# Output projection of a hybrid attention block: another pairing of the heads, and product 2 of both column blocks ahead of the rest

## The chip, the cores and the metric

The kernel runs on one core of one Trainium2 chip. The metric is the device time of one execution in microseconds (us). TensorE (PE) multiplies, VectorE (DVE) and ScalarE (ACT) do the elementwise work, GpSimd (POOL) a little masking, and SyncE (SP) issues the DMAs.

## What is computed

One layer of a hybrid encoder block in float32, for 512 tokens of width 2048: an input projection, eight heads of stick-breaking attention, eight heads of forgetting attention, a norm of each head, the output projection, and an MLP. The change lies in the output projection; cut to that, the reference is:

```python
o_sb = stick_breaking_attention(qa, ka, va)            # heads 0..7
o_fox = forgetting_attention(qf, kf, vf, log_f)        # heads 8..15
mixed = concatenate([head_rmsnorm(o_sb, g_out_sb), head_rmsnorm(o_fox, g_out_fox)], axis=-1)
x = x + einsum('bse,ed->bsd', mixed, w_out)            # (512 x 2048) @ (2048 x 2048)
h2 = rmsnorm(x, g_mlp)
u = relu(einsum('bsd,df->bsf', h2, w_up))
x = x + einsum('bsf,fd->bsd', u * u, w_down)
y = rmsnorm(x, g_final)
```

## The kernel before, in words

Every float32 product is made of three matmuls on fp32r halves (`mm3`, lines 77 to 79): high x high, high x low, low x high. The high half is a cast on ACT, the low half a subtraction on DVE (`split`, lines 59 and 60).

The large products are done as 2 x 2 blocks with seven products in place of eight (Strassen's scheme in Winograd's form), numbered 1 to 7. For the output projection the left matrix `mixed` (tokens x heads) is split into two token halves and two inner halves, and w_out into the same inner halves and two column halves. Before, the inner halves are the even heads and the odd heads: a pair `m` holds heads 2m and 2m+1. Product 1 is A11 B11 and reads the first inner half alone, product 2 is A12 B21 and reads the second half alone, product 4 also reads only the second, and products 5, 6, 7 and 3 need both or sums of them. The sums of the weights for products 4 to 7 are made during attention (`WeightSums`, line 986 loads two row blocks of w_out for each m) and kept in DRAM (`wsums`, `whigh`; the ready halves of products 1 and 2 for column block 0 in `wraws`).

The left forms are made by `g_form(p, parts)`: sums on DVE in place in `mixed`, a cast on ACT, a subtraction on DVE, over the pairs m0 to m1. They lie in tiles `G[p]` that take over rooms of the earlier input tiles; the left forms `F` of the next stage take over those rooms again (`left_form`).

A column half of 1024 is done in two column blocks of 512 (`db` 0 and 1). In each block every product runs in four pieces of two pairs (`out_piece(p, db, m0)`), 12 matmuls of 512 columns each. The weights of a piece come into a pair of buffers (high and low): three pairs in the pool `w`, and in column block 0 a fourth (`px`), in turn. For column block 0 of products 1 and 2 they are loaded ready (line 1410), for product 6 half ready (lines 1412 and 1413), for all others loaded raw (lines 1431 and 1433) and split on ACT and DVE.

The sums are gathered in three accumulators in PSUM, `A`, `B` and `C`, each of two tiles of 512. In the trace they are accoa, accob and accoc. Products 1, 6, 7 and 4 add up in one accumulator, 5 and 3 in C; `take(p, db)` (line 1453) adds an accumulator to a quarter of x on DVE after each product that ends a value, and product 6 goes on adding onto product 1 behind such a take. Before, in column block 0, A is accoa and B, for product 2, is accob; in block 1 they are exchanged. `turn_quarter` then transposes the finished quarter on TensorE (line 1460).

PSUM pools are opened and closed like a stack: in attention `acca` (two tiles of 512), `accb` (two) and the pool of the scores, whose tile `s` has 1536 floats, with one more tile of 512. For the output projection accoa, accob and accoc are opened in that order, at the same starts. The last values of the heads are summed in `accb` (`accv`), and the output and the norm sums of the last head lie in a tile `oq` of the scores' tag.

Attention runs the forgetting heads first and the stick-breaking heads last; heads 6 and 7 are the last two. Their chain at the end is: transposes of the weights (line 885), product with the values (lines 77 to 79 on `o` and `oq`), squares, norm sums (lines 956 and 957), a reciprocal root on ACT (lines 960 and 961), four operations on DVE (lines 966 to 969) which write `mixed`. Before, all that doesn't need heads 6 and 7 is product 1 and product 2 of block 0 without their piece m0 = 2 (pairs 2 and 3): six pieces, put behind steps of that chain by `issue_after`. Then the rest follows in the order 1, 2, 6, 5, 7, 3, 4.

The order inside attention is written out by hand; in the output projection it is that of the code, except that a planner puts an instruction ahead where an earlier one isn't ready by its own reckoning. On the chip each engine runs its own list in order.

Of the kernel before, what the change touches and what calls it, by code (L numbers as in the profile page):

```python
# [8 lines left out]
F32 = mybir.dt.float32  # L9
# [6 lines left out]
P = 128  # L16
NT = 512
# [3 lines left out]
NH = 8  # L21
# [16 lines left out]
def block_kernel(ctx, tc, x, g_attn, w_in, b_f, g_out_sb, g_out_fox, w_out, g_mlp, w_up, w_down, g_final, y):  # L38
# [5 lines left out]
    w_in, w_out, w_up, w_down = w_in[0], w_out[0], w_up[0], w_down[0]  # L44
# [84 lines left out]
    A_ORDER = (1, 4, 5, 6, 2, 7, 3)  # L129
    ROOMS = [f"f{c}{p}" for c in "hl" for p in A_ORDER]  # L130
# [90 lines left out]
    with ExitStack() as stage:  # L221
# [70 lines left out]
        c0, m = v_columns(order[0]), 2 * P + NH  # L292
# [82 lines left out]
        for k in range(4, K8):  # L375
            t, j = mm_at[k], k + K8
# [334 lines left out]
    mixed = mixp.tile([P, 2 * NH, NT], F32, name="mixed")  # L711
# [3 lines left out]
    with tc.tile_pool(name="att", bufs=1, side="right", reuse_waits="tile") as at, \  # L715
# [259 lines left out]
        class WeightSums:  # L975
# [4 lines left out]
            def load(self, sides=(0, 1)):  # L980
                if 0 in sides:
                    self.b = self.place()
                    self.q = [self.b[:, i] for i in range(4)]
                for s in sides:
                    src = w_out[(2 * self.m + s) * P:(2 * self.m + s + 1) * P].rearrange("p (j c) -> p j c", j=2)
                    sp.dma_start(self.b[:, 2 * s:2 * s + 2], src[:, :, self.ds[0] * NT:self.ds[0] * NT + self.n])

            def high(self, i):
# [209 lines left out]
    class form:  # L1198
        @staticmethod
        def tile(*args, tag, **kwargs):  # L1200
            return (form1 if tag in EARLY else form2).tile(*args, tag=tag, **kwargs)

    G_ORDER = (1, 2, 6, 5, 7, 3, 4)


    G = {p: [form.tile([P, NH, 2 * P], F32R, tag=ROOMS[2 * i + c], name=f"g{p}") for c in range(2)]
         for i, p in enumerate(G_ORDER)}
    F = {p: [None, None] for p in A_ORDER}

    def f_parts(p, a):  # L1210
# [31 lines left out]
    def a_form(p, c, out, s=None):  # L1242
        split(*out, a_source(p, c, s))
# [144 lines left out]
    aps, bps, cps = (ops.enter_context(tc.tile_pool(name=f"{c}ps", bufs=1, space=PSUM, reuse_waits="tile")) for c in "abc")  # L1388

    A, B, C = (q.tile([P, 2, NT], F32, name=f"acco{c}") for c, q in zip("abc", (aps, bps, cps)))  # L1390
    A, B = (A, B), (B, A)
    S_OF = xp.tile([P, NH, 2 * P], F32, tag="hr1", name="s12")
    out_rows = w_out.rearrange("(m s p) c -> s p m c", s=2, p=P)

    def g_form(p, *parts):
        for m0, m1 in parts:
            a_form(p, mixed[:, 2 * m0:2 * m1].rearrange("p (m s) n -> p m s n", s=2), [g[:, m0:m1, :] for g in G[p]])

    def parts_at(pool_, tag):
        t_ = pool_.tile([P, 2, 2 * NT], F32R, tag=tag, name="wx")  # L1400
# [5 lines left out]
    def out_piece(p, db, m0):  # L1406

        hi, lo = (w.rearrange("p (a b) -> p a b", a=2) for w in hi_lo(2 * NT))
        if db == 0 and p in (1, 2):
            begun_ = [sp.dma_start(w.bitcast(F32), wraws[p - 1][:, m0 // 2, i]) for i, w in enumerate((hi, lo))][1]  # L1410
        elif db == 0 and p == 6:
            begun_ = sp.dma_start(hi.bitcast(F32), whigh[:, m0 // 2])
            sp.dma_start(lo.bitcast(F32), wsums[:, m0 // 2, 3, db])
        else:
            raw = out_weights(p, db, m0)
            casts[0] = split(hi, lo, raw[0])
            begun_ = raw[1]
        ps = {2: B[db], 5: C, 3: C}.get(p, A[db])
        for t in range(2):
            ts = slice(t * P, (t + 1) * P)  # L1420
            for i in range(2):
                mm3(ps[:, t, :], G[p][0][:, m0 + i, ts], G[p][1][:, m0 + i, ts], hi[:, i, :], lo[:, i, :],
                    m0 + i == 4 and p in (1, 5, 2), m0 + i == 3)
        return begun_

    def out_weights(p, db, m0):
# [13 lines left out]
    def begin(t, j, db):  # L1440

        if t + j + db == 0:

            quarter[t, j] = wp.tile([P, 2, NT], F32, tag="wraw", name="x2")
        else:
            quarter[t, j] = xp.tile([P, 2, NT], F32, tag="x2", name="x2", bufs=3)
        sp.dma_start(quarter[t, j], xq[:, 2 * t:2 * t + 2, (2 * j + db) * NT:(2 * j + db + 1) * NT])

    def take(p, db):
        q, ps = {1: ((0, 0), A[db]), 5: ((1, 1), C), 6: ((0, 1), A[db]), 2: ((0, 0), B[db]), 7: ((1, 1), A[db]),  # L1450
                 3: ((0, 1), C), 4: ((1, 0), A[db])}[p]
        for t in range(2) if p == 4 else [slice(0, 2)]:
            dve.tensor_tensor(quarter[q][:, t, :], quarter[q][:, t, :], ps[:, t, :], op=ALU.add)
# [14 lines left out]
    def turn_quarter(t0, j, db):  # L1468
        n = 2 * j + db
        x_ = quarter[t0, j]  # L1470
        if hr[db][j] is None:
            hr[db][j] = xp.tile([P, 2, 2, NT], F32, tag=f"hr{j}", name="hr")
        for a in range(2):
            take_group(t0, j, db, a, turn_group(t0, j, db, a))
        sp.dma_start(xd[n][:, 2 * t0:2 * t0 + 2, :], x_)
        squares.append((t0, n, x_))
# [14 lines left out]
            F[p][db] = form.tile([P, 4, 2, 2 * P], F32R, tag=f"f{'hl'[db]}{p}", name=f"f{p}")  # L1491
        a_form(p, hr[db][j], [F[p][db][:, 2 * j:2 * j + 2, c, :] for c in range(2)])

    pending = []
    for db in range(2):
        if db == 1:
            begin(0, 0, db)
        else:

            for p in (1, 2):  # L1500
                g_form(p, (4, 8), (0, 2), (2, 3))
            with tc.issue_after(last_heads[2].ins):
                for p in (4, 5):
                    g_form(p, (4, 8), (0, 2), (2, 3))
            more_parts.append(lambda: parts_at(px, "px"))
            out_piece(1, 0, 4)
            with tc.issue_after(last_heads[3].ins):
                out_piece(1, 0, 6)
            with tc.issue_after(last_heads[2].ins):
                with tc.issue_after(last_heads[0].ins):  # L1510
                    out_piece(1, 0, 0)
                    out_piece(2, 0, 4)
                with tc.issue_after(last_heads[1].ins):
                    out_piece(2, 0, 6)
                    out_piece(2, 0, 0)
            begin(0, 0, db)
            for p in (1, 2, 4, 5):
                g_form(p, (3, 4))
            g_form(6, (4, 6), (6, 8), (0, 2), (2, 4))
            last_heads[4] = lows[0]  # L1520
        for i, p in enumerate(G_ORDER):
            for m0 in (2,) if db == 0 and p in (1, 2) else (4, 6, 0, 2):
                ins = out_piece(p, db, m0)
                if pending:

                    with tc.issue_after(casts[0].ins), tc.issue_after(lows[0].ins):
                        left_form(*pending.pop(0))
                if (db or p in (3, 4)) and m0 in (6, 2) and first_loads:

                    with tc.issue_after(ins.ins):  # L1530
                        u, k, a = first_loads.pop(0)
                        units[u].load(k, a)
                if db == 0 and p in (6, 5, 7) and m0 == 2:

                    with tc.issue_after(ins.ins):
                        begin(*{6: (0, 1), 5: (1, 1), 7: (1, 0)}[p], db)
                if db == 0 and p in (6, 5) and m0 != 4:

                    with tc.issue_after(last_heads[4].ins):
                        g_form({6: 7, 5: 3}[p], {6: (4, 8), 0: (0, 2), 2: (2, 4)}[m0])  # L1540
            if db == 0 and p == 5:
                more_parts.pop()
                px_cm.__exit__(None, None, None)
                mixp_cm.__exit__(None, None, None)
                rw = ctx.enter_context(tc.tile_pool(name="rw", bufs=5, side="right", reuse_waits="tile"))
                units += [Unit(0), Unit(1)]
            if db == 1 and p == 2:
                begin(0, 1, db)
                begin(1, 1, db)
            if db == 1 and p == 3:  # L1550
                begin(1, 0, db)
            take(p, db)
            if db == 1:
                pending += [(q, 0, j) for q in A_ORDER[2 * i:2 * i + 2] for j in range(2)]
            if len(squares) > 0:

                with ExitStack() as order_:
                    if casts[0] is not None:
                        order_.enter_context(tc.issue_after(casts[0].ins))
                    take_squares()  # L1560
            if p in (2, 7, 3):
                turn_quarter(*{2: (0, 0), 7: (1, 1), 3: (0, 1)}[p], db)
            if db == 1 and p == 6:
                left_form(1, 1, 0)
            if db == 1 and p == 3:
                left_form(1, 1, 1)
                for j in range(2):
                    left_form(2, 1, j)
                for q in (4, 5, 6):
                    left_form(q, 1, 1)  # L1570
        if db == 1:
            with tc.issue_after(lows[0].ins):
                summed[7, 1, 1] = a_source(7, hr[1][1])
            with tc.issue_after(casts[0].ins):
                begun = [units[0].parts(1), units[0].parts(2)]
            for p in (5, 7):
                units[0].sum_ahead(p)
        else:
            turn_quarter(1, 0, db)
# [583 lines left out]
```

## Time and profile before

| what | value |
|---|---|
| timed runs | 2003.61, 2003.64 and 2004.72 us; median 2003.64 |
| profiled execution | span 2002.0 us from the first to the last instruction; the page gives no time of its own beside it |
| busy | PE 1993.2, PE weight loads 1727.1, DVE 1745.6, ACT 1202.3, POOL 63.3 us |
| granted clock of TensorE | 0.999 on average |
| DMA | 423.54 MB, 212 GB/s on average |
| output projection in the trace | from 585 to 760 us |

In the rows below, the first number of a timeline is the start in us from the span's start, the second the duration. Then come the engine, the line of the kernel, the operation and the tiles (output<-inputs), the shape, how many instructions the row merges (x), and in brackets how long the engine was idle before it and who ended that. PEld is the loading of a matmul's stationary operand, SPq SyncE's queue of DMAs. A stretch row gives for each engine the busy time and the number of instructions, then the granted clock, the share of DMA time and the rate.

### The profile page before, as it was taken

To read this page: it belongs to the slowest core of one execution; us is meant where nothing else is said; L and a number is where in the kernel's file an instruction comes from. 1 tells how busy PE (TensorE), PEld (TensorE's weight loads), DVE (VectorE), ACT (ScalarE), POOL (GpSimd) and SP (SyncE) were. 2 spreads that over 40 slices of the span, in tenths; PEclk is the share of its full clock that TensorE was granted. 3 is DMA by queue.
4 is the path that set the end of the run, shared out by engine and by line. 5 is a ranking of instruction groups with operands and counts; after the bars stand their busy time and mean duration, and the time that the engine had idled before them with its cause. 6 is when DMAs were issued, how large, how long until landed. Compare 5 with 4: busy or idle time off the path is not lost.

```text
span 2002.0 us, 27075 instructions
## 1 busy us (share of the span) xinstructions
PE 1993.2 (100%) x10288; PEld 1727.1 (86%) x10288; DVE 1745.6 (87%) x1997; ACT 1202.3 (60%) x1648; POOL 63.3 (3%) x73
## 2 busy tenths in 40 slices
PE   9999999999999999999999999999999999999998
PEld 9998888888898889888888888888888888888887
DVE  7886888888878678999999999998798888988896
ACT  7544766787765566767676776766543444344344
POOL 0000011010110000000000000000000000000003
PEclk9999999999999999999999999999999999999999
DMA  7417977777668962666766666666694674674642
GB/s 262 157 65 246 292 230 212 227 225 219 212 214 279 299 221 95 200 203 199 219 184 215 199 203 201 199 211 233 245 348 165 228 279 142 239 262 171 215 163 85
DMA packets 309570, 423.54 MB, mean 212 GB/s; under 512 B 49424, under 2 KB 205376, under 8 KB 302912
## 3 DMA queue, kind: packets, MB, share of 16 engines
q1 hardware_dynamic: 308688, 419.71, 63.9%
q10 hardware_dynamic: 752, 2.11, 0.3%
q8 instruction: 81, 1.33, 0.3%
q14 instruction: 49, 0.40, 0.1%
HBM read 315.45 MB, written 96.49 MB: 206 GB/s over the span
## 4 chain that ended last, share of the span: by engine, by line
PE 100%; DVE 0%; issue 0%; DVEq 0%; ACT 0%; ACTq 0%
PE psa L1313 11%; PE accd L79 8%; PE accd L77 8%; PE accd L78 8%; PE accq L77 6%; PE accq L78 6%; PE accq L79 6%; PE psa L1311 6%; PE psc L1313 5%; PE psc L1311 3%; PE psb L1313 3%; PE psb L1311 1%; PE m L79 1%; PE m L77 1%; PE m L78 1%; PE accoa L77 1%
## 5 line engine op out<-in xcount | busy, mean ns | idle before, releaser
L1949 ACT CAST wh<-wd 128x1024 fp32r<-128x1024 f32 x126 | 125.0, 998 | 168.2 <-PE accd L79 55.3
L1835 DVE TENSOR_TENSOR wl<-wu,wh 128x1024 fp32r<-128x1024 f32 x158 | 192.6, 1219 | 12.2 <-ACT wh L1829 12.0
L77 PE MATMUL accq<-hH,wh 128*128 128x512 f32 x512 | 200.3, 391 | 0.0
L78 PE MATMUL accq<-hL,wh 128*128 128x512 f32 x512 | 199.4, 389 | 0.0
L79 PE MATMUL accq<-hH,wl 128*128 128x512 f32 x512 | 199.4, 389 | 0.0
L1829 ACT CAST wh<-wu 128x1024 fp32r<-128x1024 f32 x158 | 167.6, 1061 | 44.0 <-issue 27.9
L1313 PE MATMUL psa<-f,wh 128*128 128x512 f32 x720 | 179.0, 391 | 0.0
L79 PE MATMUL accd<-wh,uf 128*128 128x512 f32 x436 | 169.6, 389 | 0.0
L78 PE MATMUL accd<-wl,uf 128*128 128x512 f32 x436 | 169.6, 389 | 0.0
L77 PE MATMUL accd<-wh,uf 128*128 128x512 f32 x436 | 169.5, 389 | 0.0
L1313 PEld LDWEIGHTS psa<-f,wh 128*128 128x128 f32 x720 | 132.3, 188 | 25.6
L1956 DVE TENSOR_TENSOR wl<-wd,wh 128x1024 fp32r<-128x1024 f32 x126 | 143.9, 1150 | 10.6 <-ACT wh L1949 10.6
L1949 ACT CAST wx<-wd 128x1024 fp32r<-128x1024 f32 (+1 forms) x82 | 80.8, 994 | 107.4 <-PE accd L79 43.6
L1670 DVE TENSOR_TENSOR m<-m,accd 128x1024 f32<-128x1024 f32 x84 | 102.1, 1216 | 47.9 <-PE accd L79 47.9
L79 PEld LDWEIGHTS accq<-hH,wl 128*128 128x128 f32 x512 | 96.1, 188 | 20.3
L77 PEld LDWEIGHTS accq<-hH,wh 128*128 128x128 f32 x512 | 96.2, 188 | 19.0
L78 PEld LDWEIGHTS accq<-hL,wh 128*128 128x128 f32 x512 | 96.2, 188 | 18.9
L77 PE MATMUL accd<-wx,uf 128*128 128x512 f32 x284 | 110.5, 389 | 0.0
L78 PE MATMUL accd<-wx,uf 128*128 128x512 f32 x284 | 110.5, 389 | 0.0
L79 PE MATMUL accd<-wx,uf 128*128 128x512 f32 x284 | 110.5, 389 | 0.0
L1311 PEld LDWEIGHTS psa<-f,wl 128*128 128x128 f32 x720 | 96.0, 191 | 5.4
L1311 PE MATMUL psa<-f,wl 128*128 128x256 f32 x720 | 98.3, 282 | 0.0
(464 smaller groups left out, 5120.5 us busy)
## 6 DMA issues: line engine op xcount, KB each, us to landing
wu<-in_w_up_dram SPq DMA_DIRECT2D x60, 1024.0 KB, 6.5
ufd<-st SPq DMA_DIRECT2D x98, 512.0 KB, 4.2
wd<-in_w_down_dram SPq DMA_DIRECT2D x48, 1024.0 KB, 8.4
uf<-ufd SPq DMA_DIRECT2D x42, 1024.0 KB, 7.5
wraw<-in_w_in_dram SPq DMA_DIRECT2D x68, 512.0 KB, 5.7
wo<-wsums SPq DMA_DIRECT2D x28, 512.0 KB, 4.7
q<-in_w_in_dram SPq DMA_DIRECT2D x32, 384.0 KB, 5.3
wd<-in_w_down_dram SPq DMA_DIRECT2D x16, 768.0 KB, 5.8
```

The lines of the kernel that those rows point to most:

```text
L77: pe.matmul(out, sh, mh, start=first, stop=False, skip_group_check=True)
L78: pe.matmul(out, sh, ml, start=False, stop=False, skip_group_check=True)
L79: return pe.matmul(out, sl, mh, start=False, stop=last, skip_group_check=True)
L1311: ins = pe.matmul(ps[:, 2 * P:], lo[:, a, :], f_parts(p, a)[0], start=False, stop=last, skip_group_check=True)
L1313: ins = pe.matmul(ps, hi[:, a, :], f_both(p, a), start=a == PAIRS[0] and p in (1, 5), stop=last, skip_group_check=True)
L1670: dve.tensor_tensor(M[p][:, :, db, :], M[p][:, :, db, :], ps, op=ALU.add)
L1829: act.copy(rooms[k][0], srcs[k])
L1835: lows[0] = dve.tensor_tensor(lo, srcs.pop(k), hi.bitcast(F32), op=ALU.subtract)
L1949: act.copy(rooms[k + 3][0], srcs[k + 3])
L1956: dve.tensor_tensor(rooms[k + 2][1], srcs.pop(k + 2), rooms[k + 2][0].bitcast(F32), op=ALU.subtract)
```

## The change

The inner halves are now the stick-breaking heads (first) and the forgetting heads (second): pair m holds heads m and 8 + m. So product 2 (and 4) reads forgetting heads only, and product 1 stick-breaking heads only. Product 2 is done for both column blocks ahead of everything else, in accoa for block 0 and in accoc for block 1; product 1 of block 0 goes to accob, with its pairs 0 to 5 ahead of the last heads and the piece m0 = 6 (heads 6 and 7) behind them. The pieces run in the order m0 = 0, 2, 4, 6. Products 1, 6, 5, 7, 3, 4 follow. A quarter of x for block 1 takes product 2's result at once and is kept in a room of product 2's left form. The left forms of the next stage and the loads of w_up are spread over the new order.

```diff
-                    src = w_out[(2 * self.m + s) * P:(2 * self.m + s + 1) * P].rearrange("p (j c) -> p j c", j=2)
+                    src = w_out[(s * NH + self.m) * P:(s * NH + self.m + 1) * P].rearrange("p (j c) -> p j c", j=2)
...
-    G_ORDER = (1, 2, 6, 5, 7, 3, 4)
+    G_ORDER = (1, 6, 5, 7, 3, 4)
     G = {p: [form.tile([P, NH, 2 * P], F32R, tag=ROOMS[2 * i + c], name=f"g{p}") for c in range(2)]
-         for i, p in enumerate(G_ORDER)}
+         for i, p in enumerate((2, 1, 6, 5, 7, 3, 4))}
...
-    A, B = (A, B), (B, A)
+    A, B = (B, A), (A, B)
-    out_rows = w_out.rearrange("(m s p) c -> s p m c", s=2, p=P)
+    out_rows = w_out.rearrange("(s m p) c -> s p m c", s=2, p=P)
+    mixed_halves = mixed.rearrange("p (s m) n -> p m s n", s=2)
     def g_form(p, *parts):
         for m0, m1 in parts:
-            a_form(p, mixed[:, 2 * m0:2 * m1].rearrange("p (m s) n -> p m s n", s=2), [g[:, m0:m1, :] for g in G[p]])
+            a_form(p, mixed_halves[:, m0:m1], [g[:, m0:m1, :] for g in G[p]])
...
-        ps = {2: B[db], 5: C, 3: C}.get(p, A[db])
+        ps = {2: (B[0], C)[db], 5: C, 3: C}.get(p, A[db])
...
-                    m0 + i == 4 and p in (1, 5, 2), m0 + i == 3)
+                    m0 + i == 0 and p in (1, 5, 2), m0 + i == NH - 1)
...
+        elif t + j == 0:
+            quarter[t, j] = form.tile([P, 2, NT], F32, tag=ROOMS[1], name="x2")
...
-    pending = []
+    pending, kept = [], None
     for db in range(2):
         if db == 1:
-            begin(0, 0, db)
+            quarter[0, 0] = kept
+            pending += [(1, 0, j) for j in (1, 0)]
         else:
-            for p in (1, 2):
-                g_form(p, (4, 8), (0, 2), (2, 3))
+            g_form(2, (0, 4), (4, 8))
+            g_form(1, (0, 4), (4, 6))
             with tc.issue_after(last_heads[2].ins):
-                for p in (4, 5):
-                    g_form(p, (4, 8), (0, 2), (2, 3))
+                g_form(4, (0, 4), (4, 8))
+                g_form(5, (0, 4), (4, 6))
             more_parts.append(lambda: parts_at(px, "px"))
-            out_piece(1, 0, 4)
+            out_piece(2, 0, 0)
             with tc.issue_after(last_heads[3].ins):
-                out_piece(1, 0, 6)
+                out_piece(2, 0, 2)
             with tc.issue_after(last_heads[2].ins):
                 with tc.issue_after(last_heads[0].ins):
-                    out_piece(1, 0, 0)
                     out_piece(2, 0, 4)
+                    out_piece(2, 0, 6)
                 with tc.issue_after(last_heads[1].ins):
-                    out_piece(2, 0, 6)
-                    out_piece(2, 0, 0)
-            begin(0, 0, db)
-            for p in (1, 2, 4, 5):
-                g_form(p, (3, 4))
-            g_form(6, (4, 6), (6, 8), (0, 2), (2, 4))
+                    for m0 in (0, 2, 4, 6):
+                        out_piece(2, 1, m0)
+                    for m0 in (0, 2, 4):
+                        out_piece(1, 0, m0)
+            begin(0, 0, 1)
+            kept = quarter[0, 0]
+            take(2, 1)
+            begin(0, 0, 0)
+            take(2, 0)
+            for p in (1, 5):
+                g_form(p, (6, 7), (7, 8))
+            g_form(6, (0, 4), (4, 6), (6, 8))
-        for i, p in enumerate(G_ORDER):
-            for m0 in (2,) if db == 0 and p in (1, 2) else (4, 6, 0, 2):
+        for p in G_ORDER:
+            for m0 in (6,) if db == 0 and p == 1 else (0, 2, 4, 6):
                 ins = out_piece(p, db, m0)
...
-                pending += [(q, 0, j) for q in A_ORDER[2 * i:2 * i + 2] for j in range(2)]
+                pending += [(q, 0, j) for q in {1: (4, 5, 6), 6: (2, 7), 5: (3,)}.get(p, ()) for j in range(2)]
...
-            if p in (2, 7, 3):
-                turn_quarter(*{2: (0, 0), 7: (1, 1), 3: (0, 1)}[p], db)
+            if p in (1, 7, 3):
+                turn_quarter(*{1: (0, 0), 7: (1, 1), 3: (0, 1)}[p], db)
```

`last_heads` are steps of the last heads' chain: 0 the product with the values, 1 the norm sums, 2 the last values' low half on DVE, 3 the transposes. The constants that list which piece a load, a quarter of x or a form is put behind are moved to the new piece numbers in the same way.

More of the change, by code (lines that the diff above doesn't have):

```diff
@@ L1449, in take @@
     def take(p, db):
[L1450 removed]
+        q, ps = {1: ((0, 0), A[db]), 5: ((1, 1), C), 6: ((0, 1), A[db]), 2: ((0, 0), (B[0], C)[db]), 7: ((1, 1), A[db]),
                  3: ((0, 1), C), 4: ((1, 0), A[db])}[p]
@@ L1527, in block_kernel @@
                         left_form(*pending.pop(0))
-                if (db or p in (3, 4)) and m0 in (6, 2) and first_loads:
+                if (db or p in (3, 4)) and m0 in (2, 6) and first_loads:
                     with tc.issue_after(ins.ins):
@@ L1532, in block_kernel @@
                         units[u].load(k, a)
-                if db == 0 and p in (6, 5, 7) and m0 == 2:
+                if db == 0 and p in (6, 5, 7) and m0 == 6:
                     with tc.issue_after(ins.ins):
                         begin(*{6: (0, 1), 5: (1, 1), 7: (1, 0)}[p], db)
-                if db == 0 and p in (6, 5) and m0 != 4:
+                if db == 0 and p in (6, 5) and m0 != 0:
                     with tc.issue_after(last_heads[4].ins):
-                        g_form({6: 7, 5: 3}[p], {6: (4, 8), 0: (0, 2), 2: (2, 4)}[m0])
+                        g_form({6: 7, 5: 3}[p], {2: (0, 4), 4: (4, 6), 6: (6, 8)}[m0])
             if db == 0 and p == 5:
@@ L1546, in block_kernel @@
                 units += [Unit(0), Unit(1)]
-            if db == 1 and p == 2:
+            if db == 1 and p == 1:
                 begin(0, 1, db)
```

## The prediction

> **What bounds the kernel now.** I read the page first (span, busy shares, clock, chain of waits), then the busy time of the engines in five stretches of the output projection, then the timeline of TensorE there.
>
> ```profile
> span 2002.0 us, 27075 instructions
> ...
> PE 1993.2 (100%) x10288; PEld 1727.1 (86%) x10288; DVE 1745.6 (87%) x1997; ACT 1202.3 (60%) x1648; POOL 63.3 (3%) x73
> ...
> PEclk9999999999999999999999999999999999999999
> ...
> PE 100%; DVE 0%; issue 0%; DVEq 0%; ACT 0%; ACTq 0%
> ```
>
> TensorE is busy for 1993.2 of 2002.0 us at full clock, and the chain that ended last is TensorE alone. The ends of its records are modelled, so I check by the starts. In an undisturbed stretch of the output projection the first and the last of 70 matmul rows are:
>
> ```profile
> 639.63 0.39 PE L77 MATMUL accoa<-wh,g 128*128 128x512 f32 x1
> ...
> 655.27 0.40 PE L77 MATMUL accoc<-wh,g 128*128 128x512 f32 x1
> ```
>
> That is 15.64 us for 69 steps, 0.2267 us each, so a weight piece (12 matmuls) costs 2.72 us. The stretches of the output projection:
>
> ```profile
> core 0: us, PE busy (x) PEld busy (x) DVE busy (x) ACT busy (x) POOL busy (x), PEclk, DMA share, GB/s
> 585.00:611.00 26.00, 26.00 (x145) 22.76 (x145) 19.17 (x30) 11.97 (x20) 1.52 (x2) 1.00 0.73 248
> 611.00:640.00 29.00, 29.00 (x133) 23.88 (x132) 26.20 (x33) 16.83 (x28) 0.00 (x0) 1.00 0.82 289
> 640.00:686.00 46.00, 46.00 (x217) 38.30 (x216) 24.22 (x22) 24.89 (x42) 0.00 (x0) 1.00 0.94 300
> 686.00:720.00 34.00, 34.00 (x156) 28.24 (x155) 29.96 (x36) 20.80 (x29) 0.00 (x0) 1.00 0.86 277
> 720.00:760.00 40.00, 40.00 (x214) 34.42 (x213) 30.68 (x35) 26.46 (x45) 0.00 (x0) 1.00 0.49 161
> ```
>
> TensorE has no gap in any of them; VectorE is at 90% (26.20 of 29.00) in the second. The place that the change is about, the end of the last two heads:
>
> ```profile
> 604.34 0.39 PE L79 MATMUL accob<-wh,g 128*128 128x512 f32 x1
> 604.56 0.39 PE L957 MATMUL ssq<-n,onesr 128*128 128x512 f32 x1
> ...
> 605.01 0.39 PE L957 MATMUL oq<-pl,onesr 128*128 128x512 f32 x1
> 605.24 0.39 PE L77 MATMUL accob<-wx,g 128*128 128x512 f32 x1
> ...
> 609.22 0.68 DVE L966 SCALAR_TENSOR_TENSOR ph<-oq,ra_last 128x512 f32<-128x512 f32 x1
> 609.82 0.42 DVE L60 TENSOR_TENSOR g<-mixed,g 128x256 fp32r<-128x256 f32 x1
> ...
> 610.68 0.39 PE L77 MATMUL accoa<-wh,g 128*128 128x512 f32 x1
> 611.60 0.75 DVE L969 SCALAR_TENSOR_TENSOR mixed<-os_last,g_rest,ph 128x512 f32<-128x512 f32 x1
> ```
>
> After the norm sums (605.24) two pieces cover the norm chain, and the first matmul that needs head 6 starts at 610.68, 0.44 us after its form is ready (609.82 + 0.42). The cover is short, but it is enough: nothing is waited for. So more cover has nothing to win. What is left to ask is whether the new order makes TensorE wait.
>
> **The change part by part.**
>
> *Same work.* Pieces before: 7 products x 2 column blocks x 4 = 56. After: 8 (product 2, both blocks) + 3 + 1 (product 1, block 0) + 5 x 4 + 6 x 4 = 56. Matmuls, transposes, DMAs and their sizes stay; the heads of a pair only have other rows of w_out. The forms of the left side fall from 26 pairs of cast and subtraction to 21 with the same elements. Price 0; VectorE saves under 1 us, which is off the path.
>
> *Cover for the last heads.* 11 pieces instead of 6 stand ahead of them, 5 x 2.72 = 13.6 us more. Gain 0, by the row at 610.68 above. At most the 0.44 us of slack turns out to be a wait in other runs.
>
> *Product 1, then product 6, on one accumulator.* Product 6 adds onto the bank pair of product 1, and product 1 must have been read out (`take`) in between. Before, product 2 ran in that place on another pair. After, product 6 follows at once in both column blocks. The take, as it stands now:
>
> ```profile
> 613.86 0.39 PE L79 MATMUL accoa<-wh,g 128*128 128x512 f32 x1
> 614.28 1.22 DVE L1453 TENSOR_TENSOR x<-x,accoa 128x1024 f32<-128x1024 f32 x1 [0.70 <-PE accoa L79]
> ...
> 627.67 0.39 PE L79 MATMUL accoa<-wh,g 128*128 128x512 f32 x1
> 630.03 1.21 DVE L1453 TENSOR_TENSOR x<-x,accoa 128x1024 f32<-128x1024 f32 x1
> ...
> 649.61 0.39 PE L79 MATMUL accoa<-wh,g 128*128 128x512 f32 x1
> 650.04 1.22 DVE L1453 TENSOR_TENSOR x<-x,accoa 128x1024 f32<-128x1024 f32 x1 [0.41 <-PE accoa L79]
> ```
>
> With VectorE free, the accumulator is open again at 614.28 + 1.22 = 615.50, and TensorE could have gone on at 613.86 + 0.23 = 614.09: 1.41 us. At 649.61 it is 1.42, and at 627.67, where VectorE is crowded, 3.34. Other TensorE work to fill it: the pieces behind are product 6 on the same pair; product 5 (accumulator c) comes four pieces later, and its weights have no free buffer (three pairs in block 1, four in block 0). The transposes of that quarter wait for the same take. So in block 1 the price is 1.4 to 1.8, I take 1.5, the free row plus 0.1 for the restart. In block 0 it is 0 (pieces of product 2 still left over to fill it) to 3.3 (crowded VectorE); I take 1.5, the rows that are nearest.
>
> *Product 2 of column block 1 in accumulator c.* By the order of the pools, a, b and c take the banks of `acca`, `accb` and the first two of the score tile, and that score tile holds the last head's output and norm sums (`oq`). Its last reader is the row at 609.22: c is open from 609.90, while these four pieces are written to follow the norm sums (605.24 on TensorE, the same as before, since the two pieces ahead are replaced by two others). Only product 1 (accumulator b) can fill 605.24 to 609.90. It stands behind product 2 for the weight buffers. Bounds: 0, if two of its pieces have weights in time (5.44 us), and 4.66, if the buffers are held by product 2. Between them, weights of product 1 go in when a buffer pair is freed by the first piece after the last heads' products, as SyncE does it now:
>
> ```profile
> 601.58 0.32 SPq L1410 DMA_DIRECT2D wl<-wraws  x1
> 601.99 0.38 SPq L1410 DMA_DIRECT2D wh<-wraws  x1
> 604.53 0.32 SPq L1410 DMA_DIRECT2D wl<-wraws  x1
> ...
> wh<-wraws SPq DMA_DIRECT2D x6, 512.0 KB, 4.4
> ```
>
> 601.99 + 4.4 = 606.4, a wait of 1.2 us. The next pair comes 2.9 us later (604.53), about as fast as TensorE uses one. I take 1.2.
>
> *ACT and VectorE.* Four splits (cast and subtraction) come from block 1 to the tail. They stand behind the heads' chain only if the order puts them ahead; TensorE has 13.6 us more work there, which covers 4 x 1.2 us. Taken as 0, bound 2.
>
> *Accumulator c for product 5.* It needs take(2) of block 1 first, and that needs its quarter of x, which now lies in the room of a half of product 2's left side and loads only after the last matmul of product 2:
>
> ```profile
> x<-in_x_dram SPq DMA_DIRECT2D x8, 512.0 KB, 6.1
> ```
>
> 0.4 for the issue (as for the weights above) + 6.1 + 1.2 for the take = 7.7 us, against four pieces of product 6, 10.9 us. Hidden, with 3.2 to spare; what waits behind it in SyncE's queue (weights of product 6) is covered by filled buffers. 0, bound 2.
>
> *Left forms.* 14 as before, at one a piece. Those of product 4 need the room in which that quarter of x lies until its squares are done, so they come two or three pieces later and then in a bunch; 0, bound 2. *Loads of w_up* end with product 4's last piece instead of product 3's:
>
> ```profile
> 734.87 3.03 SPq L1433 DMA_DIRECT2D wo<-wsums  x2
> ...
> 755.22 1.27 DVE L1453 TENSOR_TENSOR x<-x,accob 128x512 f32<-128x512 f32 x2
> ```
>
> The last weights are issued by 737.9, the last take is at 755.22: 17 us of room. 0.
>
> **Sum.** 1.5 + 1.5 + 1.2 = 4.2 us onto the profiled span: 2006.2. The timed median, 2003.64, is 1.64 above that span; 2006.2 + 1.64 = **2007.8 us**. About 0.2%, or 4.0 us, is what a measurement of this kernel can tell from no change, so this lies on the edge.
>
> **Rivals.**
>
> 1. *One stall only*: block 0's take is filled by left-over pieces, and product 1's weights are in time. 1.5 us: 2005.1. For it: SyncE's loads of product 1 need no ACT and may take a free buffer first. Chance 0.20. With all three hidden, no change (2003.6): 0.05, since in block 1 no piece is free to fill the gap.
>
> 2. *The whole wait for c*: product 2 holds all buffers. 1.5 + 1.5 + 4.66 = 7.7: 2011.3. For it: they stand first in the code. Chance 0.23. Such a wait could also cost clock. At the start, after idling, this trace has slow matmuls:
>
> ```profile
> 1.58 1.65 PE L305 MATMUL vx<-still 128*128 128x256 f32 x6 [1.58 <-DVE still L301]
> ...
> 5.79 0.81 PE L311 MATMUL vy<-wh,hH 128*128 128x264 f32 x2
> 6.39 0.64 PE L311 MATMUL vz<-wh,hH 128*128 128x264 f32 x2
> ...
> 7.30 0.48 PE L311 MATMUL vy<-wl,hH 128*128 128x264 f32 x2
> 7.62 0.40 PE L311 MATMUL vz<-wl,hH 128*128 128x264 f32 x2
> ```
>
> 0.30 us a matmul at 5.79 against 0.16 at 7.30: half rate for some 5 us from 1.58, a loss of 2.5. That would give 2013.8; 0.03 of the 0.23. The page shows clock 9 throughout, so the rate of the rows decides. The Trainium skill (TensorE: Matmul & The Clock Gate, Part 1) says that an idle window of about 3.4 us halves the clock until a busy window of the same length has passed; by that figure an estimate of the loss is 1.7 us, and no wait of that length stands in this trace behind its start.
>
> 3. *VectorE or SyncE slips further* (product 5 late in c, forms in a bunch): 2 us more than the forecast, 2010. Against it the slack above. Chance 0.05.
>
> 4. *Faster*: the modelled records hide weight waits that the deeper cover takes away. Weight loads are busy for 38.30 of 46.00 us in the third stretch. If the 17% outside them were waits, and the 11 pieces ahead of the last heads lost theirs, 29.9 x 0.17 = 5.0 us: 1998.6. It decides from about 9 such pieces on. Against it the 70 rows: every step is 0.2267, and a wait would be uneven. Chance 0.03. The Trainium skill (Perfetto Trace Analysis, Identifying the Most-Contended Engine) holds busy matmul rows to be a bad measure and takes the busy share of weight loads instead; by that rule the page's 86% would be room, and by the even steps it is not.
>
> **How the numbers follow.** The forecast has 0.44. Its spread is 2006 to 2009.6, of which somewhat over half lies above 2007.6 (0.27); with rivals 2 and 3 slower has 0.55. The rest of it, one stall, and no change give the same time: 0.42. Faster: 0.03. The range, 2004.9 to 2012.5, leaves out the no-change and faster cases and the lost clock.
>
> **What would show it.** In the changed profile: a step of about 1.6 us between the last matmul of product 1 and the first of product 6 on accumulator a in block 1, with a `take` row (L1453's successor) in it; the same on b in block 0; a gap on TensorE after the second norm sum of the last head, with the first row on c not ahead of the last reader of `oq`; elsewhere even steps of 0.2267. The prediction is wrong if the order of TensorE's rows puts work on c or b into those places, or if weights of product 1 are there at 605.

## The result and the profile after

| kernel | median, us | range, us | runs | ratio to before, 95% interval |
|---|---|---|---|---|
| before | 2004.18 | 2003.61 to 2004.99 | 4 | |
| after | 2021.75 | 2021.29 to 2023.09 | 4 | 1.0089 [1.0075, 1.0103] |

The change costs 17.6 us. The forecast was 2007.8, with 2012.5 as the upper end: the sign was right, the size was not. (One profiled execution further down, of the first run with the take ahead, took 5173 us with matmuls at less than half rate from its start to its end; only that run's timed executions are used.)

The page of the kernel after, its first lines, the clock and the chain of waits:

```profile
span 2021.4 us, 27072 instructions
...
PE 1998.3 (99%) x10288; PEld 1729.8 (86%) x10288; DVE 1745.7 (86%) x1991; ACT 1202.2 (59%) x1643; POOL 64.2 (3%) x73
...
PEclk9999999999998999999999999999999999999999
...
PE 96%; DVE 2%; DMA 2%; ACT 0%; issue 0%; SPq 0%; DVEq 0%; ACTq 0%
```

As many matmuls as before, 10288, but TensorE is no longer the whole chain: VectorE and DMA have 2% each, and one slice of the clock is at 8. The view of waits says what TensorE waited for, the three largest first (us in total, times, longest):

```profile
PE accoc L77 <- DVE ph L966: 8.1, 1, 8.1
PE psa L77 <- DVE x L1454: 3.3, 1, 3.3
PE tr L1461 <- DVE x L1454: 2.7, 2, 1.4
```

Three groups, all for VectorE; before, none of them was there. The first on the timeline of TensorE:

```profile
606.04 0.39 PE L957 MATMUL oq<-pl,onesr 128*128 128x512 f32 x1
614.48 0.77 PE L77 MATMUL accoc<-wx,g 128*128 128x512 f32 x1 [8.05 <-DVE ph L966]
...
618.88 0.39 PE L78 MATMUL accoc<-wx,g 128*128 128x512 f32 x1
```

The first column is the start. From the last norm sum to the first row of product 2 of column block 1 there are 8.44 us, 8.21 more than a step. The ten steps that follow, 614.48 to 618.88, take 4.40 us in place of 2.27: half rate, 2.1 us lost. The same stretch by windows (span, busy times, then the granted clock) confirms that it is the clock, 0.61 to 0.65:

```profile
606.00:615.00 9.00, 0.95 (x3) 0.51 (x3) 8.90 (x14) 3.96 (x7) 0.00 (x0) 0.65 0.39 117
615.00:620.00 5.00, 5.00 (x15) 3.91 (x14) 4.40 (x9) 2.28 (x5) 0.00 (x0) 0.61 0.00 0
```

In the first window VectorE is busy for 8.90 of 9.00 us. What it does there, from its timeline:

```profile
606.81 1.21 DVE L1454 TENSOR_TENSOR x<-x,accoa 128x1024 f32<-128x1024 f32 x1
607.94 1.22 DVE L60 TENSOR_TENSOR wl<-wo,wh 128x1024 fp32r<-128x1024 f32 x1
609.07 1.82 DVE L1233 TENSOR_TENSOR mixed<-mixed 128x1024 f32<-128x1024 f32 x2
610.81 0.68 DVE L966 SCALAR_TENSOR_TENSOR n<-ssq,ra 128x512 f32<-128x512 f32 x1
...
613.65 0.68 DVE L966 SCALAR_TENSOR_TENSOR ph<-oq,ra_last 128x512 f32<-128x512 f32 x1
```

The last row is the last reader of `oq`, whose banks accumulator c takes. Before, it started at 609.22, 4.2 us after the last norm sum; now 7.6 us after it. Ahead of the two heads' chains stand the take of product 2 of column block 0, the low half of a weight piece and the sums for product 6. The weights of the waiting piece were not late: their low half was written by 599.6.

The other places: product 1 to product 6 in both column blocks, and a place that the prediction does not have, the first product of the up stage (the product with w_up):

```profile
638.19 0.39 PE L79 MATMUL accob<-wh,g 128*128 128x512 f32 x1
639.89 1.09 PE L1461 MATMUL tr<-ident,x 128*128 128x128 f32 x8 [1.31 <-DVE x L1454]
...
708.62 0.39 PE L79 MATMUL accoa<-wh,g 128*128 128x512 f32 x1
710.41 1.07 PE L1461 MATMUL tr<-ident,x 128*128 128x128 f32 x8 [1.41 <-DVE x L1454]
...
767.34 0.39 PE L79 MATMUL accoa<-wh,g 128*128 128x512 f32 x1
770.99 0.36 PE L77 MATMUL psa<-f,wh 128*128 128x256 f32 x1 [3.26 <-DVE x L1454]
...
772.51 0.41 PE L77 MATMUL psa<-f,wh 128*128 128x256 f32 x1
...
775.91 0.28 PE L77 MATMUL psb<-f,wh 128*128 128x256 f32 x1
...
778.43 1.03 PE L1461 MATMUL tr<-ident,x 128*128 128x128 f32 x8
```

Less one step of 0.23 each, they are 1.47, 1.56 and 3.42 us. From 772.51 to 775.91 another 16 steps take 3.40 us in place of 1.9: 1.5 us of clock. The last row, the last transposes of the output projection, ends a stage that all these kernels share; I measure it from the last norm sum on `oq` to here. Before it ran from 605.01 to

```profile
759.07 1.04 PE L1460 MATMUL tr<-ident,x 128*128 128x128 f32 x8
```

154.06 us; after, 778.43 - 606.04 = 172.39. The difference, 18.3, is the sum of the pieces: 8.21 + 2.1 + 1.47 + 1.56 + 3.42 + 1.5. Behind this stage both profiles need the same (1242.9 and 1243.0 us to the end of the span); the remaining 1.0 of the 19.4 us between the spans lies ahead of it, in small slips of the first stages. I use the length of this stage to compare single executions, since the timed runs of one kernel with such waits lie 1 to 3 us apart.

### The profile page after: what moved, and what is told of

Same layout as the page of the kernel before. It is cut to its first block, busy times and chain, and to the rows that moved or that the text cites. A ratio compares the mean times of both kernels' runs of the same rounds, so it can differ in the third digit from the quotient of the medians.

```text
span 2021.4 us, 27072 instructions
## 1 busy us (share of the span) xinstructions
PE 1998.3 (99%) x10288; PEld 1729.8 (86%) x10288; DVE 1745.7 (86%) x1991; ACT 1202.2 (59%) x1643; POOL 64.2 (3%) x73
## 4 chain that ended last, share of the span: by engine, by line
PE 96%; DVE 2%; DMA 2%; ACT 0%; issue 0%; SPq 0%; DVEq 0%; ACTq 0%
PE psa L1311 11%; PE accd L79 8%; PE accd L78 8%; PE accd L77 8%; PE psa L1309 6%; PE psc L1311 5%; PE accq L77 5%; PE accq L79 5%; PE accq L78 5%; PE psc L1309 3%; PE psb L1311 3%; PE psb L1309 1%; PE m L78 1%; PE m L79 1%; PE m L77 1%; PE accoc L77 1%
```

## Experiments

The theory after the two traces: three accumulators lie on banks whose last reader is late. Accumulator c waits for `oq`, and that wait is long since VectorE has other work ahead of the heads' chain; product 6 waits for the take of product 1; and with A and B exchanged, product 4 of column block 1 ends on the banks of psa, the first accumulator of the up stage. Two of these waits also cost clock. The rivals: late weights, a VectorE that is simply too full, the other pairing as such.

**Product 1 first.**

```
-  for m0 in (0, 2, 4, 6): out_piece(2, 1, m0)
   for m0 in (0, 2, 4): out_piece(1, 0, m0)
+  for m0 in (0, 2, 4, 6): out_piece(2, 1, m0)
```

> The kernel after, with the two short loops behind the last norm sums exchanged: three pieces of product 1 (accumulator b, 3 x 2.72 = 8.2 us) stand ahead of the four pieces of product 2 of column block 1 (accumulator c). Theory 'the bank': the 8.05 us wait is for the last reader of the score tile whose banks accumulator c takes, and the slow matmuls behind it (10 rows at 0.43 us in place of 0.227, 2.1 us) come from that idle time. Then both go: 2021.75 - 8.2 - 2.1 = 2011.4, or up to 2012.6 if the first weights of product 1 come 1.2 us late; the wait for the accumulator is under 0.5 us. Rival 'the weights': what is late is SyncE and ACT with the weights of whatever comes next; then the wait only moves to accumulator b, and the time stays within 2018 to 2022.

Measured: 2015.50 us (2012.91 to 2015.79, 5 runs), ratio 1.0053 [1.0041, 1.0066]; the stage takes 163.25 us, 9.1 less than after. The row behind the last norm sum (606.54) is on accumulator b at 606.77, one step later: the wait for c is gone, and the weights of product 1 were in time too. The rival, whose wait only moves to b, falls. The median is 2.9 us above the upper forecast of 2012.6; in the profiled execution (2014.44 us) the stage is 1.2 short of the 10.3 us. That is at the next take:

```profile
628.30 0.39 PE L79 MATMUL accob<-wh,g 128*128 128x512 f32 x1
631.13 1.09 PE L1461 MATMUL tr<-ident,x 128*128 128x128 f32 x8 [2.44 <-DVE x L1454]
631.98 0.48 PE L77 MATMUL accob<-wx,g 128*128 128x512 f32 x1
...
632.60 0.63 PE L79 MATMUL accob<-wx,g 128*128 128x512 f32 x1
...
635.94 0.40 PE L78 MATMUL accob<-wx,g 128*128 128x512 f32 x1
```

The wait is 2.60 us net, 1.1 more than after, since sums for products 7 and 3 now stand ahead of the take on VectorE; and 8 slow steps follow, 3.34 us in place of 1.8. In exchange the wait at psa, still 3.41 us, had no slow rows behind it in this execution; whether the slower timed runs had them is not shown.

**psa on other banks.**

```
-  self.A, self.C, self.B = (... for c in "acb")
+  self.B, self.C, self.A = (... for c in "bca")
```

> The kernel after, with the three accumulators of the first up units made in another order, so that psa lies on the banks of accumulator c (free since product 3) and not on those of accumulator a, in which product 4 ends. Theory 'the bank': the 3.4 us wait at the first psa row goes, and with it the 16 matmuls at 0.2125 us in place of 0.118 (1.5 us): 2021.75 - 3.4 - 1.5 = 2016.8. If the slow rows have another cause and stay: 2018.3. Rival 'VectorE': the queue of VectorE is full there, so the time is lost at the next product (its low half of weights or its forms): no wait at psa but 3 us more of waits in the next 20 us, 2020 to 2022.

Measured: 2018.38 us (2017.04 to 2019.80, 5 runs), ratio 1.0071 [1.0058, 1.0083]; the stage takes 167.92, 4.5 less.

```profile
766.36 0.39 PE L79 MATMUL accoa<-wh,g 128*128 128x512 f32 x1
766.59 0.28 PE L77 MATMUL psa<-f,wh 128*128 128x256 f32 x1
...
770.00 0.36 PE L1315 MATMUL psb<-f,wh 128*128 128x256 f32 x1 [0.39 <-DVE x L1454]
```

psa follows in one step; psb, the second accumulator of the up stage and now on accumulator a's banks, waits 0.4 (0.5 by the starts). There are no slow rows behind psa. By its median alone this would be the forecast in which the slow rows stay, 2018.3; the rows decide, and show wait and slow rows gone together. VectorE is no emptier: from 760 to 775 it is busy for 14.20 of 15.00 us, after for 12.86. So the rival falls.

**The same bank in the kernel before.**

```
-  self.A, self.C, self.B = (... for c in "acb")
+  self.C, self.A, self.B = (... for c in "cab")
```

> The kernel before, with one line changed: psa of the up stage lies on the banks in which product 4 of column block 1 ends (there accumulator b). Nothing of the heads or the products is touched. Theory 'the bank': the first psa row must wait for the take of product 4 (3.2 to 3.4 us), and the rows behind it run at half rate for about as long (1.5 us): 2004.1 + 4.9 = 2009.0. If only the wait counts: 2007.4. Rival 'VectorE': the 3.3 us of the kernel after come from a queue that is fuller there; then the take of before, with no such queue, costs 1.4 us and no clock: 2005.5.

Measured: 2009.87 us (2008.71 to 2011.48, 8 runs), ratio 1.0029 [1.0019, 1.0040]; the stage takes 159.02, 5.0 more than before.

```profile
752.64 0.39 PE L79 MATMUL accob<-wh,g 128*128 128x512 f32 x1
756.32 0.36 PE L77 MATMUL psa<-f,wh 128*128 128x256 f32 x1 [3.29 <-DVE x L1453]
...
757.71 0.41 PE L79 MATMUL psa<-f,wl 128*128 128x256 f32 x1
...
761.12 0.28 PE L79 MATMUL psb<-f,wl 128*128 128x256 f32 x1
```

One line, nothing of heads or products touched, gives the whole term: 3.45 us of wait and 16 slow steps over 3.41 us. The rival (1.4 us with an emptier VectorE) falls. The median is 0.9 above the 2009.0 forecast; in the profile, the first accumulator of the down stage (the product with w_down) waits 1.0 us more with this layout.

**A piece between product 1 and product 6.** In column block 1 the first piece of product 5 (accumulator c) is moved behind the last of product 1.

```
+  if db == 1 and p == 1: pieces.append((5, 0))
+  if db == 1 and p == 5: pieces.pop(0)
```

> The kernel after, with the first weight piece of product 5 (accumulator c, 2.72 us) moved between product 1 and product 6 of column block 1 (accumulator a). Theory: the step from the last matmul of product 1 to the transposes, 1.56 us net, is the take that nothing covers; a piece on another accumulator covers it: 2021.75 - 1.5 = 2020.2. Rival: the take is then delayed behind the low half of the extra piece's weights, or the next stall between products takes it over: 2021.75 within 0.5 us.

Measured: 2021.15 us (2020.61 to 2022.21, 4 runs), ratio 1.0085 [1.0072, 1.0099]; the stage takes 171.58, 0.8 less. By its time alone this is nearer the rival. The rows tell it better:

```profile
710.87 0.39 PE L79 MATMUL accoc<-wh,g 128*128 128x512 f32 x1
711.11 1.03 PE L1461 MATMUL tr<-ident,x 128*128 128x128 f32 x8
...
765.26 0.39 PE L79 MATMUL accoa<-wh,g 128*128 128x512 f32 x1
768.95 0.55 PE L77 MATMUL psa<-f,wh 128*128 128x256 f32 x1 [3.29 <-DVE x L1454]
...
775.02 0.28 PE L77 MATMUL psb<-f,wh 128*128 128x256 f32 x1
```

The stall is covered: from the piece to the transposes it is one step. From the norm sum to the first psa row the kernel is 1.9 us faster than after (163.01 against 164.95): 1.56 of it is the stall, the rest a shorter slow stretch behind the wait for c. But behind psa the slow rows last 6.1 us here, up to 775.02, not 3.4, and give 1.1 us back. What a wait costs in clock is not a constant; the last section returns to it.

**Filling the wait.** After the norm sums, 32 matmuls on accumulator b whose values are overwritten.

```
+  for n in range(32):
+      pe.matmul(A[0][:, n % 2, :], onesr, G[2][0][:, 0:2, :], start=True, stop=True, ...)
```

> The kernel after, with 32 more matmuls (32 x 0.227 = 7.25 us, of 512 columns, on accumulator b, whose values are overwritten later) between the last norm sums and product 2 of column block 1. They do nothing but keep TensorE busy during the wait for accumulator c. Theory 'idle time costs clock': the wait ends at the same time (614.5 in the profile), but the 10 matmuls behind it run at 0.227 and not 0.43: 2021.75 - 2.1 = 2019.7. Rival: the matmuls behind the wait are slow because their weights or the accumulator come late, not by the clock: 2021.75, and the rows behind it stay at 0.43. If the fill delays the wait's end (VectorE and ACT do not depend on it) the time rises by at most 0.5.

Measured: 2020.39 us (2018.50 to 2021.36, 5 runs), ratio 1.0080 [1.0066, 1.0094]; the stage takes 170.31, 2.1 less.

```profile
605.41 7.42 PE L1517 MATMUL accob<-g,onesr 128*128 128x512 f32 x32
613.63 0.47 PE L77 MATMUL accoc<-wx,g 128*128 128x512 f32 x1 [0.80 <-DVE ph L966]
```

The wait ends 8.4 us after the norm sums, as in the kernel after; the rows behind it step by 0.23 from the second on, and the granted clock is 1.00 from 605 to 619, where it was 0.61 to 0.65. So the 2.1 us were the clock, and idle time was its cause.

**The heads' chain ahead of take and sums.**

```
+  with tc.issue_after(last_heads[5].ins):      # last row of the heads' norm chains
       take(2, 0)
 ...
+  with tc.issue_after(last_heads[5].ins):
       g_form(6, (0, 4), (4, 6), (6, 8))
```

> The kernel after, with the take of product 2 of column block 0 (1.21 us) and the sums for product 6 (1.82 us) put behind the last head's norm chain in VectorE's queue; before they stood ahead of it. Theory: the wait for accumulator c is as long as it is because VectorE works on these first. Its chain then starts when ACT has its root, 608.1 and not 610.8 in the profile's times, so the wait falls from 8.05 to 5.3 us and the time to 2021.75 - 2.7 = 2019.0; the slow rows behind it stay. Rival: ACT, or the weights of product 2, hold the chain too: the wait falls by under 1 us, 2021 to 2022.

Measured: 2019.34 us (2018.80 to 2019.65, 5 runs), ratio 1.0075 [1.0062, 1.0088]. In the view of waits:

```profile
PE accoc L77 <- DVE ph L966: 5.4, 1, 5.4
```

8.1 to 5.4 us, as expected: 2.7 of the wait were two jobs that VectorE could have done later. What is left is the chain itself and a weight piece: its cast (605.43) stands ahead of the root on ACT, so the chain starts 2.1 us after the last norm sum (607.76), 1.4 before the change. That the median comes so near 2019.0 is partly chance: the profiled execution (2019.43 us) had no slow rows behind psa, which cost 1.5 us in the kernel after.

**The pairing alone.** The kernel before with the halves of the other pairing, product 2 of column block 1 left on its own accumulator and in its place (its order of pieces in block 0 is 2, 2, 2, 1, norm sums, 1, 1, 1, 2). A and B are exchanged as in the change, and psa lies on b's banks, which are free there.

```
-  src = w_out[(2 * self.m + s) * P : ...]        +  src = w_out[(s * NH + self.m) * P : ...]
-  out_rows "(m s p) c -> s p m c"                +  out_rows "(s m p) c -> s p m c"
...
```

> The other pairing of the heads alone: the kernel before with inner halves of the stick-breaking and the forgetting heads, product 2 of column block 1 in its old place on its own accumulator, product 2 of column block 0 ahead of product 1 with its last piece kept for the take of product 1, and psa on banks that are free. Theory: the pairing costs nothing, all the loss is in the order of the products and the banks; no wait of over 0.6 us in the output projection: 2004.1, within 1. Rival: the other rows of the weights or the forms cost time themselves: above 2006. Rival: what is freed at the last heads was hidden work and gains: 2003 or less.

Measured: 2008.40 us (2008.08 to 2009.29, 11 runs), ratio 1.0022 [1.0013, 1.0031]; the stage takes 156.89, 2.8 more than before. The theory said nothing over 0.6 us; it is wrong by this row:

```profile
611.64 0.39 PE L79 MATMUL accob<-wh,g 128*128 128x512 f32 x1
613.89 0.50 PE L77 MATMUL accob<-wh,g 128*128 128x512 f32 x1 [1.87 <-ACT g L59]
...
1388.10 0.47 PE L77 MATMUL accd<-wh,uf 128*128 128x512 f32 x1 [1.05 <-DVE l L1349]
```

TensorE waits 2.0 us for a head's form; the other 0.8 are small slips behind it. In the old pairing product 1 needs the first of the last two heads and product 2 the second; in the new one both are in product 1, so its last piece waits for the second chain (ACT casts the first of these forms at 609.84, this one at 613.43). The pairing thus needs more cover than the two pieces that stand there: what the change's other half brings. The last row is the down stage's first accumulator, which this layout of psa, psb and psc makes wait: another 1.4 us from the last transposes to the end of the span (1244.3 against 1242.9). The weights' rows and the forms as such cost nothing that these rows show.

**All four waits mended.** Product 1 first; in block 0 the last piece of product 2 of column block 1, in block 1 the first of product 5, between products 1 and 6; psa on b's banks.

> The kernel after with its four waits taken away: product 1 ahead of product 2 of column block 1; the last piece of that product 2 between product 1 and product 6 of column block 0; the first piece of product 5 between those of column block 1; psa on banks that are free (those of accumulator b). Theory: what remains is the time of before: 2004.1, within 1.5; no wait of over 0.6 us between the last norm sums and the up stage. Rival: the waits come back at other places, as in the run with product 1 first, where the take of product 1 took 1.1 us longer: 2006 to 2009. Rival: deeper cover gains: under 2003.

Measured: 2008.86 us (2007.13 to 2010.13, 11 runs), ratio 1.0023 [1.0014, 1.0032]; the stage takes 156.30. Of the 18.3 us 16.1 are gone. The rival with its waits elsewhere has the rest: the take of product 1 in block 0 outlasts its cover, behind the 4.8 us of sums on VectorE that the first experiment met, and the down stage waits as above:

```profile
PE tr L1461 <- DVE x L1454: 2.2, 1, 2.2
...
PE accd L77 <- DMA uf<-ufd: 1.0, 1, 1.0
```

**The take ahead of the sums**, in the kernel with all four waits mended, and psa on c's banks.

```
+  taken = take(p, db)
+  if db == 0 and p == 1: last_heads[4] = taken     # sums for products 7 and 3 follow it
```

> The kernel with all four waits mended, with the two places at which it still lost time: the take of product 1 of column block 0 stands ahead of the sums and forms for products 7 and 3 in VectorE's queue (there 4.8 us of such sums stood ahead of it, and TensorE waited 2.2 us), and psa lies on the banks of accumulator c with psb on those of a (the layout on b's banks made the first accumulator of the down stage wait 1.0 us more, 1.3 in the stage). Theory: nothing else is left of the loss: 2004.0 + 0.4 for a short wait at psb = 2004.4, within 1. Rival: the sums put back make product 7 or 3 wait for its form: 2006 or more. Rival: the deeper cover gains: 2003 or less.

Measured, 11 timed runs: 2005.81 to 2010.51, median 2008.32; ratio 1.0023 [1.0014, 1.0032]. That is 3.9 us over the forecast. By its time alone it is the first rival, a late form.

> The kernel with the take ahead once more, for a profile of an execution at the ordinary speed (the profiled execution of the run before took 5173 us, with matmuls at well under half rate from the first to the last; its timed ones 2005.8 to 2010.5). Theory: somewhere behind product 6 a form for product 7 or 3, put back behind the take, is late, by about 4 us in all: a wait of TensorE for a row of ACT or VectorE that writes such a form. Rival: no wait of over 0.6 us is in the output projection, and the 4 us lie outside it, in the up or down stage.

Measured: 2008.75 us (2006.48 to 2009.26, 8 runs), ratio 1.0023 [1.0011, 1.0034]; the stage takes 158.99, 4.9 more than before. Both mended places are gone (the transposes at 627.03 follow in one step, and from the last transposes to the end it needs 1243.0 us again), psb waits 0.6 us, and a new wait has come within product 6 of block 0:

```profile
635.85 0.39 PE L79 MATMUL accob<-wh,g 128*128 128x512 f32 x1
638.91 0.77 PE L77 MATMUL accob<-wh,g 128*128 128x512 f32 x1 [2.67 <-ACT x L1489]
```

The busy time by windows (the last two columns are the share of the DMA engines and GB/s), and a row of its DMA issues (median us from issue to landing):

```profile
600.00:620.00 20.00, 20.00 (x89) 16.54 (x89) 17.74 (x24) 11.44 (x18) 0.00 (x0) 1.00 0.57 189
620.00:640.00 20.00, 17.33 (x79) 14.12 (x78) 16.76 (x21) 9.39 (x17) 0.00 (x0) 0.97 0.95 336
```

```profile
wh<-whigh SPq DMA_DIRECT2D x3, 512.0 KB, 8.5
```

It is 2.8 us, and 1.5 of clock behind it; with psb that is the 4.9. Neither theory named it: not a form, and inside the output projection. ACT's squares, which the view names, write nothing that product 6 reads; its last weights were issued at 628.78 for 1.48 us, and with 8.5 us to landing (5.3 in the kernel before) they are there at 637.3 to 638.8. The DMA engines are busy for 95% of 620 to 640, 57% in the 20 us ahead; in the kernel before it is 83% and 75%. That the weights are what is late is argued from these rows and was not tried.

No version beats the kernel before.

## Why the prediction was wrong

Of the 18.3 us, 10.3 are the wait for accumulator c with its clock (forecast: 1.2), 4.9 are psa with its clock (no term), and 3.0 are the two takes (forecast: 3.0). So one term was far too small and one was missing.

- *Product 1, then product 6, on one accumulator*: 1.5 + 1.5 forecast, 1.47 + 1.56 measured, both with a take row in the gap. Right for block 1. In block 0 it is partly luck: VectorE was free there because the wait for c had held TensorE back.

```profile
638.61 1.22 DVE L1454 TENSOR_TENSOR x<-x,accob 128x1024 f32<-128x1024 f32 x1 [3.48 <-PE accob L79]
```

  With that wait gone, the same take cost 2.60 us (product 1 first), nearer the crowded 3.3.
- *Product 2 of column block 1 in accumulator c*: the mechanism and the place were right, the size failed: 1.2 taken, 4.66 as the upper bound, 8.21 measured. Two steps failed. The first took weights of product 1 into a freed buffer pair by 606.4; they were issued only at 619.54, as SyncE had given the buffers to product 2, and TensorE's list has product 1 behind all of product 2 (first row at 627.53).

```profile
619.54 0.80 SPq L1409 DMA_DIRECT2D wx<-wraws  x2
```

  The second is the bound: it kept the last reader of `oq` at its old 609.22, as if nothing else of the change touched VectorE.
- *ACT and VectorE*, priced 0 with a bound of 2: this is the step that broke that bound. The text named the condition ("only if the order puts them ahead") and then answered with 13.6 us of cover, but seven of the eleven pieces that were to cover stand behind the very wait. And it priced only the four splits. Of the three jobs right ahead of the chain on VectorE one is such a split (607.94, 1.22 us); the take of product 2 and the sums for product 6 stand in no term, and the run with the chain first prices these two at 2.7 us. Without them the wait is 5.52 us, 0.9 over the bound.
- *The clock*: only in a rival, with 0.03. That rival's price, 2.5 us, was near the 2.1 measured, but its chance was tied to the 4.66 us wait.
- *A missing term*: A and B are exchanged in the diff, so that product 4 of column block 1 ends on the banks of psa. The prediction followed the last take (755.22) for the loads of w_up and not for its bank. 3.42 us of wait and 1.5 of clock, a quarter of the loss; the one-line change of the kernel before shows it alone.
- *Cover for the last heads*, gain 0: right for the old pairing. In the new pairing more cover is needed: with two pieces behind the norm sums the run with the pairing alone waits 2.0 us.
- *Accumulator c for product 5, left forms, loads of w_up*, all 0: no wait for them is in the view of waits. Right.
- Rival 2 with lost clock, 2013.8, came nearest. With the measured 8.21 in place of 4.66 and 2.1 in place of 2.5 it would give 2017; the rest is psa.

## What to carry to other kernels

When accumulators are renamed or moved, follow each bank pair to its last reader in the stage ahead and to its next user in the stage behind, across pool boundaries too. A bound on a wait for a reader holds only if nothing that the change moves stands ahead of that reader in its engine's queue: list the queue in its new order first. And work that is meant to cover a wait must be able to start before it; pieces queued behind the waiting instruction cover nothing.

## What the runs showed of the hardware

A wait of TensorE costs clock by where it falls. Slow stretches begin and end on a grid of about 3.41 us. Behind psa one lasts 3.40 us after, and 3.41 in the kernel before with psa on b. After, one slow stretch ends at 618.88, the next starts at 772.51, 45.0 periods of 3.413 us later, and ends one period on. In the run with the piece between, the ends at 617.94 and 775.02 are 46.0 apart. The grid lies elsewhere in each execution: divided by 3.413, the first end leaves 1.1 us after, 0.2 with the piece between, and the one of the fill (772.03) 0.7. The Trainium skill (TensorE: Matmul & The Clock Gate, Part 1) states such a window, free-running, of 3413 ns; the traces agree.

They disagree on what sets the slow state off, if an idle window is one without any matmul. The Trainium skill asks for one idle window, but TensorE was never idle for a whole one at psa. I count the busy share of each grid window from the rows, transposes included. The next window was slow after shares of 16, 21, 41, 41 and 44% (the fill, the piece between, product 1 first at its take, the kernel before with psa on b, after), and after 21% in the second run with the take ahead. It was fast after 46 to 48% (the chain first and product 1 first, both at psa). Transposes have to be counted: at the take of column block 1, after, the window is 54% busy with them and 35% without, and the next one is fast, while 41 and 44% of matmuls alone were not enough. Once slow, a window at 64 or 78% did not end it, and one at 96% and full ones did. So the same wait of 3.4 us at psa cost 0 (chain first, product 1 first), 1.5 (after, fill, before with psa on b) or 2.7 us (piece between), and even 2.6 us of wait with transposes behind it cost 1.5.

How busy a window must be rests on these few windows, and no run was set up for it. The ends of slow stretches are read to a step of 0.1 to 0.2 us, 3 to 6% of a window, so the limit can only be put at some 40 to 50%.
